# A four-layer decoder trunk: residual stream token-major, output products in 512-column matmuls

## The chip, the core and the metric

The kernel runs on one core of a Trainium2 chip. The metric is the device time of one execution in microseconds (us), lower is better. The engines are TensorE (PE, with its weight loads listed as PEld), VectorE (DVE), ScalarE (ACT), GpSimd (POOL) and SyncE (SP); here SP's queue issues the DMAs that bring the weights.

## The reference

A batch of one, 256 tokens, model width 1024, four layers, all in float32. Each layer has a token mixer (0: gMLP, 1: multi-head latent attention, MLA, 2: HGRN2, 3: gMLP again) and a convolutional FFN (2816 wide). A conditioning vector c gives every layer six vectors of 1024: shift, scale and gate for the mixer and for the FFN (adaLN).

```python
def rmsnorm(x, g):
    y = x * lax.rsqrt(jnp.mean(x * x, axis=-1, keepdims=True) + EPS)
    return y * g
...
for i in range(DEPTH):
    mod = c_act @ ada_w[i] + ada_b[i]
    sh1, sc1, g1, sh2, sc2, g2 = jnp.split(mod, 6, axis=-1)
    h = modulate(rmsnorm(x, mix_norm_g[i]), sh1, sc1)     # h * (1 + sc) + sh
    y = gmlp_mixer / mla_mixer / hgrn2_mixer (h, ...)     # each ends in "@ w_out"
    x = x + (1.0 + g1)[:, None, :] * y
    h = modulate(rmsnorm(x, ffn_norm_g[i]), sh2, sc2)
    x = x + (1.0 + g2)[:, None, :] * conv_ffn(h, ...)     # ends in "@ w_down"
return rmsnorm(x, final_g)
```

The last product of a mixer (go in gMLP, wo in MLA and HGRN2) and of an FFN (dn) is called an output product here: 1024 columns wide, with 2048, 1024 or 2816 rows to sum over. It is followed by the gate, the residual sum and the next norm.

## The kernel before, in words

The residual stream `x` lies feature-major: 128 partitions x 8 chunks of 128 features x 256 tokens. Every product is done in split form: a float32 operand is a high part in TensorE's fp32r type plus a low part, and `mm3` issues three matmuls (high by high, high by low, low by high; L239 to L241). Weights arrive as `raw` tiles of mostly 1 MB on SP's queue (`unit`, `want`, `dma_next`); ACT casts them to `wh` (L208) and DVE subtracts for `wl` (L209), 1024 columns at a time.

An output product of before takes weights of 128x128 as stationary operand and lets the 256 tokens move past. For each of the eight chunks of 128 output features a PSUM tile is finished, and `residual` (L458) does x += gate * product on DVE (L460), with the gate as a number for each partition. `square_chunk` squares the new chunk on ACT (L428; the last chunk on DVE, L426), and `stat_add` (L399) sums over features on TensorE, by short matmuls against ones into the tile `st`. When all eight are in, `rms_bc` (L407) takes the root (L409) and the reciprocal (L411), spreads the result over the partitions by TensorE (`bcn`, L416), and `modulate_chunk` (L440) makes the next product's operand `hh` and `hlo` chunk by chunk (DVE L444, ACT L445, DVE L446). The dn weights come as three pieces along the rows to sum over (8, 8 and 6 chunks of 128).

The adaLN vectors come in two ways, spread over the whole kernel as filler work: `ada_vector` (multiply and sum on DVE, L316) and `ada_tensor` (16 short matmuls `adaps` for a block, L294). `pacing` decides from the table RATE and from the count of units done how many of these steps each stage takes; `need` forces those that are wanted next. Blocks on TensorE that are still loaded run in the gap of a norm (`while loaded["p"]: ada_run("p")` in `modulated`).

The order of instructions on each engine is not the order of the source: a list scheduler with its own cost estimates sets it, within what the buffers allow (5 `raw` tiles, 10 of the pool "big", 3 "misc" and 4 "acc" PSUM banks). Engines then run their queues in order.

The stages in order: v, u, go (gMLP, layer 0), up, dn (FFN 0), MLA with wo, up, dn, HGRN2 with wo, up, dn, v, u, go (layer 3), up, dn, and the final norm. In what follows the gap ahead of a stage is the time from the last matmul of an output product to the first of the next product: up0 is the gap between go and up of layer 0, mix1 the one between dn of layer 0 and the mixer of layer 1, and so on.

Of the kernel before, what the change touches and what calls it, by code (L numbers as in the profile page):

```python
# [8 lines left out]
F32 = mybir.dt.float32  # L9
# [6 lines left out]
PSUM = bass.MemoryType.PSUM  # L16

# [17 lines left out]
OUTS = ((0, 0, 4), (0, 4, 4), (1, 0, 4), (1, 4, 4))  # L35
CONVAT = (3,)
SQACT = [3, 7]
# [9 lines left out]
STLAG = 3  # L47
# [4 lines left out]
        ("dn", 0): (0.0, 0.8), ("mix", 1): (1.85, 0.6), ("up", 1): (0.0, 0.2), ("dn", 1): (0.0, 0.85),  # L52
        ("mix", 2): (0.0, 0.4), ("lev", 2): (0.0, 0.25), ("hout", 2): (0.25, 1.05), ("up", 2): (0.0, 0.15),
        ("dn", 2): (0.0, 1.0), ("mix", 3): (0.0, 0.5), ("u", 3): (0.0, 0.3), ("go", 3): (0.0, 0.5),
        ("up", 3): (0.35, 0.0), ("dn", 3): (0.0, 0.7)}
# [6 lines left out]
for _name, _w in (("mix_g", 32), ("ada_b", 192), ("ffn_g", 32), ("final_g", 8), ("qg", 2), ("kvg", 1),  # L62
                  ("gmlb", 32), ("lb", 32), ("hgn", 1)):
    _COLS[_name] = _n
    _n += _w
# [27 lines left out]
def build(ctx, tc, A, out, stages=None):  # L93
# [8 lines left out]
    pp = ctx.enter_context(tc.tile_pool(name="pp", bufs=1, space=PSUM))  # L102

# [19 lines left out]
    x = one.tile([P, KC, S], F32, name="x")  # L123
    prm = one.tile([P, NPRM], F32, name="prm")
    for i in range(2):
        nc.sync.dma_start(x[:, 4 * i : 4 * i + 4, :], A["x"][:, 4 * i : 4 * i + 4, :])
    cin = one.tile([P, 8], F32, name="cin")
    nc.scalar.dma_start(cin[:], A["c"])
    n0, n1 = _COLS["ada_b"] + 48, _COLS["lb"]
# [3 lines left out]
    ident = one.tile([P, P], F32, name="ident")  # L133
# [3 lines left out]
    def late_consts():  # L137
        with tc.issue_after(state["lastdma"]):
            nc.sync.dma_start(prm[:, n1:], A["prm"][:, n1:])
            nc.sync.dma_start(ident[:], A["ident"])  # L140
# [12 lines left out]
    act.activation(cact[:], cin[:], AF.Silu)  # L153
# [94 lines left out]
    gate = one.tile([P, L, 2, 8], F32, name="gate")  # L248

    def mod_post(l, b0, n):  # L250
# [7 lines left out]
        elif part in (2, 5):  # L258
            dve.tensor_scalar_add(gate[:, l, part // 5, c : c + n], m, 1.0)
# [119 lines left out]
    def pacing():  # L379
# [3 lines left out]
        flush()  # L383
        for m in "pd":
# [22 lines left out]
    def rms_bc(ps, n, name, pieces=1):  # L407
# [5 lines left out]
        bc = [misc(f"bc{name}", (P, S // pieces)) for i in range(pieces)]  # L413
        for j in range(4):
            i, o = divmod(64 * j, S // pieces)
            pe.matmul(bc[i][:, o : o + 64], sel[:, j : j + 1].broadcast_to([P, P]), rs[:], start=True, stop=True)  # L416
        return bc[0] if pieces == 1 else bc

    cur = {"sq": []}

    def square_chunk(c):
        if c == 0:
            cur["st"] = stat_new("st")
        sq = t1("sq")[:]
        if c == KC - 1:
            dve.tensor_tensor(sq, x[:, c, :], x[:, c, :], op=ALU.mult)  # L426
        else:
            act.activation(sq, x[:, c, :], AF.Square)  # L428
        if c == 0:

            act.activation(sm("warm", 1)[:], sq[:, 0:1], AF.Sqrt)
        cur["sq"].append((sq, c))
        while len(cur["sq"]) > (STLAG if c < KC - 1 else 0):
            sq, i = cur["sq"].pop(0)
            stat_add(cur["st"], sq, i == 0, i == KC - 1)
# [4 lines left out]
    def modulate_chunk(l, which, c, bc):  # L440
        b = 24 * which + c
        sh = mod[:, l, b : b + 1]
        t = t1("nt")
        dve.scalar_tensor_tensor(t[:], x[:, c, :], amul[:, l, which, c : c + 1], bc, op0=ALU.mult, op1=ALU.mult)  # L444
        act.activation(hh[:, c, :], t[:], AF.Identity, bias=sh)  # L445
        dve.scalar_tensor_tensor(hlo[:, c, :], t[:], sh, hh[:, c, :].bitcast(F32), op0=ALU.add, op1=ALU.subtract)  # L446

    def modulated(l, which):
        bc = rms_bc(cur["st"], D, f"n{l}{which}")
# [3 lines left out]
        for c in range(KC):  # L453
            modulate_chunk(l, which, c, bc[:])
            if c in CONVAT:
                conv_half()

    def residual(l, which, c, ps):  # L458
        need(l, 2 + 3 * which)
        dve.scalar_tensor_tensor(x[:, c, :], ps, gate[:, l, which, c : c + 1], x[:, c, :], op0=ALU.mult, op1=ALU.add)  # L460
        square_chunk(c)
# [4 lines left out]

    def pair(name, apart):

        if apart:
            return [acc(f"{name}a", (P, S))[:], misc(f"{name}b", (P, S))[:]]  # L470
        t = acc(name, (P, 2, S))
        return [t[:, 0, :], t[:, 1, :]]
# [84 lines left out]
    def gmlp(l, j, start=None):  # L557
# [289 lines left out]
    class OutProj:  # L847


        def __init__(self, l, yh, yl):  # L850
            self.l, self.yh, self.yl = l, yh, yl
            self.ps = None

        def step(self, i):
            w = unit(LAST if i == 3 else None)
            if i == 0:
                self.ps = [v for t in range(4) for v in pair(f"wo{t}", False)]
            order = [(k, t) for k in range(2) for t in range(8)] if i < 3 else [(k, t) for t in range(8) for k in range(2)]
# [457 lines left out]
```

## Time and profile before

| | |
|---|---|
| runs of before | 1374.18 us median of 3 (1372.25 to 1375.31) |
| the profiled execution | 1373.39 us, span of its profile 1371.7 us |
| DMA | 326.22 MB, 238 GB/s over the span |
| instructions | 29075 |

The span is the stretch from the first to the last instruction in the profile; 1.7 us of the execution lie around it. In a row of the groups (line, engine, operation, out<-in, shapes, count) the first number behind the bar is the group's busy time, the second the mean of one in ns, and behind the next bar stands the idle time of the engine just before them and what ended it. In a row of the timeline the first number is the start in us, the second the duration; matmul durations overlap, so their pitch is read from the starts. Neighbours of one kind are joined in one row with a count.

### The profile page before, as it was taken

To read this page: it belongs to the slowest core of one execution; us is meant where nothing else is said; L and a number is where in the kernel's file an instruction comes from. 1 tells how busy PE (TensorE), PEld (TensorE's weight loads), DVE (VectorE), ACT (ScalarE), POOL (GpSimd) and SP (SyncE) were. 2 spreads that over 40 slices of the span, in tenths; PEclk is the share of its full clock that TensorE was granted. 3 is DMA by queue.
4 is the path that set the end of the run, shared out by engine and by line. 5 is a ranking of instruction groups with operands and counts; after the bars stand their busy time and mean duration, and the time that the engine had idled before them with its cause. 6 is when DMAs were issued, how large, how long until landed. Compare 5 with 4: busy or idle time off the path is not lost.

```text
span 1371.7 us, 29075 instructions
## 1 busy us (share of the span) xinstructions
PE 1339.3 (98%) x12244; PEld 1280.1 (93%) x12244; DVE 1107.8 (81%) x1788; ACT 770.8 (56%) x1202; POOL 17.0 (1%) x19
## 2 busy tenths in 40 slices
PE   8999999999999999999998999999999999999997
PEld 6799999999898899999897899999987999999997
DVE  5699788889787698897789978889877864888843
ACT  3764366664466666654666546665356543666633
POOL 0100000000000000000000000000001000000000
PEclk9999999999999999999999999999999999999999
DMA  9869955557957366588573756558958464455531
GB/s 383 333 246 336 386 203 192 197 211 314 382 214 278 117 253 215 228 317 348 204 258 125 297 222 247 212 181 325 361 186 303 176 234 164 158 181 184 185 124 32
DMA packets 49484, 326.22 MB, mean 238 GB/s; under 512 B 5957, under 2 KB 9029, under 8 KB 11975
## 3 DMA queue, kind: packets, MB, share of 16 engines
q1 hardware_dynamic: 47568, 322.72, 62.8%
q8 instruction: 96, 1.57, 0.5%
q10 hardware_dynamic: 1784, 1.65, 0.4%
q14 instruction: 36, 0.29, 0.1%
HBM read 323.29 MB, written 1.05 MB: 236 GB/s over the span
## 4 chain that ended last, share of the span: by engine, by line
PE 91%; DVE 4%; ACT 3%; DMA 1%; issue 1%; SPq 0%; DVEq 0%; ACTq 0%
PE up L240 12%; PE up L239 12%; PE up L241 12%; PE dn L239 5%; PE dn L240 5%; PE dn L241 5%; PE go L239 2%; PE go L240 2%; PE go L241 2%; PE u L240 2%; PE u L239 2%; PE u L241 2%; PE v L239 2%; PE v L240 2%; PE v L241 2%; DMA adaf<-ada 1%
## 5 line engine op out<-in xcount | busy, mean ns | idle before, releaser
L208 ACT CAST wh<-raw 128x1024 fp32r<-128x1024 f32 x426 | 434.8, 1032 | 390.2 <-PE up L240 170.9
L209 DVE TENSOR_TENSOR wl<-raw,wh 128x1024 fp32r<-128x1024 f32 x426 | 513.0, 1210 | 145.4 <-ACT wh L208 143.7
L239 PE MATMUL up<-hh,wh 128*128 128x256 f32 x1408 | 397.5, 283 | 2.6 <-ACT hh L445 2.5
L241 PE MATMUL up<-hh,wl 128*128 128x256 f32 x1408 | 397.4, 283 | 0.0
L240 PE MATMUL up<-hlo,wh 128*128 128x256 f32 x1408 | 397.3, 283 | 0.1
L239 PEld LDWEIGHTS up<-hh,wh 128*128 128x128 f32 x1408 | 269.7, 192 | 4.9 <-ACT hh L445 4.5
L240 PEld LDWEIGHTS up<-hlo,wh 128*128 128x128 f32 x1408 | 269.7, 192 | 0.6 <-DVE hlo L446 0.5
L241 PEld LDWEIGHTS up<-hh,wl 128*128 128x128 f32 x1408 | 270.0, 192 | 0.0
L316 DVE CUSTOM_DVE_ANT_0 adaw<-adaw,cbc,prm 128x1024 f32<-128x1024 f32 x120 | 152.1, 1278 | 2.3 <-DMA adaw<-adad 2.1
L239 PE MATMUL dn<-gh,wh 128*128 128x256 f32 x528 | 150.0, 284 | 3.0 <-ACT y L1095 3.0
L240 PE MATMUL dn<-gl,wh 128*128 128x256 f32 x528 | 149.4, 283 | 0.0
L241 PE MATMUL dn<-gh,wl 128*128 128x256 f32 x528 | 149.4, 283 | 0.0
L1095 ACT ACTIVATE y<-up,cwb 128x256 f32<-128x256 f32 x176 | 98.7, 561 | 11.4 <-DVE y L1097 11.3
L239 PEld LDWEIGHTS dn<-gh,wh 128*128 128x128 f32 x528 | 101.3, 192 | 3.7 <-ACT y L1095 3.3
L240 PEld LDWEIGHTS dn<-gl,wh 128*128 128x128 f32 x528 | 101.3, 192 | 0.0
L241 PEld LDWEIGHTS dn<-gh,wl 128*128 128x128 f32 x528 | 101.3, 192 | 0.0
L1097 DVE SCALAR_TENSOR_TENSOR y<-up,cwb,y 128x254 f32<-128x254 f32 x176 | 84.6, 481 | 4.8
L1096 DVE SCALAR_TENSOR_TENSOR y<-up,cwb,y 128x255 f32<-128x255 f32 x176 | 83.9, 477 | 0.5 <-ACT y L1095 0.4
L239 PE MATMUL u<-hh,wh 128*128 128x256 f32 x256 | 74.0, 289 | 0.0
L239 PE MATMUL go<-yh,wh 128*128 128x256 f32 x256 | 73.3, 287 | 0.0
L241 PE MATMUL u<-hh,wl 128*128 128x256 f32 x256 | 72.4, 283 | 0.0
L240 PE MATMUL u<-hlo,wh 128*128 128x256 f32 x256 | 72.4, 283 | 0.0
(340 smaller groups left out, 2457.4 us busy)
## 6 DMA issues: line engine op xcount, KB each, us to landing
raw<-up SPq DMA_DIRECT2D x88, 1024.0 KB, 4.8
adaw<-adad SPq DMA_DIRECT2D x60, 1024.0 KB, 7.0
raw<-dn SPq DMA_DIRECT2D x32, 1024.0 KB, 4.9
adaw<-adap SPq DMA_DIRECT2D x28, 1024.0 KB, 7.8
raw<-gmu SPq DMA_DIRECT2D x16, 1024.0 KB, 6.3
raw<-gmo SPq DMA_DIRECT2D x16, 1024.0 KB, 4.8
raw<-gmv SPq DMA_DIRECT2D x15, 1024.0 KB, 8.9
raw<-dn SPq DMA_DIRECT2D x16, 768.0 KB, 8.4
```

The lines of the kernel that those rows point to most:

```text
L208: act.copy(wh[:, :w], raw[:, o : o + w])
L209: i = dve.tensor_tensor(wl[:, :w], raw[:, o : o + w], wh[:, :w].bitcast(F32), op=ALU.subtract)
L239: pe.matmul(ps, lh, rh, start=start, stop=False)
L240: pe.matmul(ps, lh, rl, start=False, stop=False)
L241: i = pe.matmul(ps, ll, rh, start=False, stop=stop)
L316: dve.tensor_tensor_reduce(raw[:, e, :], raw[:, e, :], cbc[:], 1.0, prm[:, c0 : c0 + 1], ALU.mult, ALU.add, mod[:, l, b : b + 1])
L1095: act.activation(y[:], ps[:, e, :], AF.Identity, bias=b, scale=w[2])
L1096: dve.scalar_tensor_tensor(y[:, 1:], ps[:, e, : S - 1], w[1], y[:, 1:], op0=ALU.mult, op1=ALU.add)
L1097: dve.scalar_tensor_tensor(y[:, 2:], ps[:, e, : S - 2], w[0], y[:, 2:], op0=ALU.mult, op1=ALU.add)
```

## The change

The residual stream becomes token-major: `x` is 128 partitions (tokens) x 2 token halves t x 1024 features.

- Output products (`out_product`): 128x128 blocks of activations (features x 128 tokens) are stationary, and 512 weight columns move. The four combinations of token half t and column half f have a PSUM bank each. In all units but the last the loop runs over the weight chunks with t and f inside; in the last unit it finishes one (t, f) after the other. The weights of go and dn are packed for it; dn now has 11 units of 1 MB (8 of 1 MB and 4 of 0.75 MB before), and its paces in RATE are scaled to that. In the last dn the final two units are merged.
- Gates: a gate is now a row along the features and has to stand on all partitions. `gate_row` puts the gate's 8 columns into a cleared tile (POOL), adds one, transposes blocks of 32x32 (both DVE) and stores the result by four DMAs of 8x32 to device memory; `gate_load` reads it back, spread over 128 partitions, into the tile `gx` (pool "big").
- `residual(t, f)`: DVE multiplies 512 columns by the gate (`gated`) and adds them to x; ACT squares with its accumulator, which gives the sum of squares for each token. After f = 1: `root` (ACT square root and DVE reciprocal of one column) and `scaled` (x times the reciprocal root into `gx`, half on DVE, half on ACT).
- `turned`: 16 transposes of 128x128 on TensorE put the scaled x back feature-major, into PSUM tiles `xt`; `modulate_chunk` reads them. The matmuls `st` and `bcn` of these norms go away.
- The final norm multiplies by a row of final_g loaded by a DMA; the first norm uses accumulators of ACT and DVE; `ident` is loaded at the start.

```diff
+    def gate_row(l, which, m):
+        g = t1("gcol", 32)
+        pool.memset(g[:], 0.0)
+        dve.tensor_scalar_add(g[:, 0:8], m, 1.0)
+        r = t1("grow", 32)
+        dve.transpose(r[:], g[:])
+        row = dp.tile([8, 4, 32], F32, name=f"gate{l}{which}")
+        for j in range(4):
+            nc.sync.dma_start(row[:, j, :], r[32 * j : 32 * j + 8, :])
+        grows[l, which] = row
...
+        gx = cur["gx"] = big("gx", (P, 2, D))
+        row = grows.pop((l, which))
+        nc.sync.dma_start(gx[:, 1, :], row[:].rearrange("c j i -> (c j i)").unsqueeze(0).broadcast_to([P, D]))
...
+    def scaled(t, rs):
+        xn = cur["gx"][:, t, :]
+        dve.tensor_scalar_mul(xn[:, 0:512], x[:, t, 0:512], rs)
+        i = act.activation(xn[:, 512:D], x[:, t, 512:D], AF.Copy, scale=rs)
...
+    def turned(c, w, bank=misc):
+        ps = bank("xt", (P, w, S))
+        for e in range(w):
+            for t in range(2):
+                pe.transpose(ps[:, e, t * P : t * P + P], cur["gx"][:, t, (c + e) * P : (c + e) * P + P], ident[:])
+        return ps
...
-        dve.scalar_tensor_tensor(t[:], x[:, c, :], amul[:, l, which, c : c + 1], bc, op0=ALU.mult, op1=ALU.mult)
-        act.activation(hh[:, c, :], t[:], AF.Identity, bias=sh)
-        dve.scalar_tensor_tensor(hlo[:, c, :], t[:], sh, hh[:, c, :].bitcast(F32), op0=ALU.add, op1=ALU.subtract)
+        dve.tensor_scalar(t[:], xt, amul[:, l, which, c : c + 1], mod[:, l, b : b + 1], op0=ALU.mult, op1=ALU.add)
+        split(hh[:, c, :], hlo[:, c, :], t[:])
...
-    def residual(l, which, c, ps):
-        need(l, 2 + 3 * which)
-        dve.scalar_tensor_tensor(x[:, c, :], ps, gate[:, l, which, c : c + 1], x[:, c, :], op0=ALU.mult, op1=ALU.add)
-        square_chunk(c)
+    def residual(t, f, ps, last):
...
+        dve.tensor_tensor(g[:], ps, gx[:, 1, s], op=ALU.mult)
+        dve.tensor_tensor(x[:, t, s], x[:, t, s], g[:], op=ALU.add)
+        act.activation(g[:], x[:, t, s], AF.Square, accum_out=ss[:, 2 * t + f : 2 * t + f + 1])
...
+        if f == 0:
+            if t == 0:
+                act.activation(sm("warm", 1)[:], ss[:, 0:1], AF.Sqrt)
+            dve.tensor_scalar(ss[:, 4 + t : 5 + t], ss[:, 2 * t : 2 * t + 1], 1.0 / D, EPS, op0=ALU.mult, op1=ALU.add)
+        else:
+            rs = root(t, ss[:, 6:8], ss[:, 2 * t + 1 : 2 * t + 2], ss[:, 4 + t : 5 + t])
...
+                scaled(t, rs)
...
+    def out_product(name, k0, units, yh, yl, last, fin_=False):
...
+        def one_(kc, t, f):
+            a, b = hl(units[(kc - k0) // 2], kc % 2 * D + 512 * f, 512)
+            ts = slice(t * P, t * P + P)
+            mm3(ps[2 * t + f][:], yh(kc)[:, ts], yl(kc)[:, ts], a, b, kc == 0, kc == last)
...
         pace("go", l)
+        gate_load(l, 0)
         for i in range(8):
             w = unit(LAST if i == 7 else None)
-            ps = acc(f"go{i}", (P, S))
-            for k in range(16):
-                a, b = hl(w, k * P, P)
-                mm3(ps[:], a, b, yh(k), yl(k), k == 0, k == 15)
-                if k == 7:
-                    flush(mid=1)
-            residual(l, 0, i, ps[:])
+            out_product("go", 2 * i, [w], yh, yl, 15)
```

How the change moves instructions shows at three places. The first is DVE at the end of go in layer 0 (in the rows: `x<-go` and `gated<-go` are residual steps, `wl<-raw` weight conversions, `nt` and `hlo` the norm's output, `adaw,mod` an adaLN step; numbers behind names count the tiles). Before, from the last weights of go to the first nt:

```order
L209 TENSOR_TENSOR wl_0_1920<-raw_1849,wh_0_1919 128x1024
L209 TENSOR_TENSOR wl_1024_1924<-raw_1849,wh_1024_1923 128x1024
L209 TENSOR_TENSOR wl_0_1989<-raw_1917,wh_0_1988 128x1024
L460 SCALAR_TENSOR_TENSOR x<-go_1930,gate,x 128x256
L209 TENSOR_TENSOR wl_1024_1993<-raw_1917,wh_1024_1992 128x1024
L460 SCALAR_TENSOR_TENSOR x<-go_1996,gate,x 128x256
L426 TENSOR_TENSOR sq<-x 128x256
L411 RECIPROCAL rsn_2072<-sdn_2070 128x64
L209 TENSOR_TENSOR wl_0_2120<-raw_1986,wh_0_2119 128x1024
L444 SCALAR_TENSOR_TENSOR nt<-x,amul,bcn_2074 128x256
```

And in the changed kernel, in two pieces that leave out rows between:

```order
L500 TENSOR_TENSOR gated<-go_1517,gx 128x512
L210 TENSOR_TENSOR wl_0_1773<-raw_1733,wh_0_1772 128x1024
L210 TENSOR_TENSOR wl_1024_1777<-raw_1733,wh_1024_1776 128x1024
L501 TENSOR_TENSOR x<-x,gated 128x512
L500 TENSOR_TENSOR gated<-go_1518,gx 128x512
```

```order
L501 TENSOR_TENSOR x<-x,gated 128x512
L448 RECIPROCAL ss<-ss 128x1
L509 TENSOR_SCALAR ss<-ss 128x1
L455 TENSOR_SCALAR gx<-x,ss 128x512
L448 RECIPROCAL ss<-ss 128x1
L455 TENSOR_SCALAR gx<-x,ss 128x512
L339 ISA adaw_0_0_1931,mod<-adaw_0_0_1931,cbc,prm 128x1024
L339 ISA mod 128x1
L473 TENSOR_SCALAR nt<-xt,amul,mod 128x256 x3
```

The residual steps, spread over the stage before, now all stand at its end; the two conversions of the first up weights stand between the first `gated` and its `x`, and an adaLN step stands ahead of the first nt.

The second place is TensorE at the same point. Before, from the last matmul of go to the first of up:

```order
L241 MATMUL go_1996<-yh_885,wl_1024_1924 128x256
L401 MATMUL st<-sq,ones 32x64 x12
L294 MATMUL adaps<-adaw_5_0_1518,cact 32x256 x5
L401 MATMUL st<-sq,ones 32x64 x4
L294 MATMUL adaps<-adaw_5_0_1518,cact 32x256 x3
L294 MATMUL adaps<-adaw_5_1_1591,cact 32x256 x5
L416 MATMUL bcn_2074<-rsn_2072,sel 128x64 x4
L294 MATMUL adaps<-adaw_5_1_1591,cact 32x256 x3
L294 MATMUL adaps<-adaw_5_2_1657,cact 32x256 x8
L239 MATMUL up_2153<-hh,wh_0_1988 128x256
```

And after:

```order
L241 MATMUL go_1520<-wl_1024_1740,yh_869 128x512
L242 MATMUL go_1520<-wh_1024_1739,yl_870 128x512
L464 MATMUL xt<-ident,gx 128x128 x16
L240 MATMUL up_1933<-hh,wh_0_1772 128x256
L240 MATMUL up_2005<-hh,wh_0_1899 128x256
```

The adaLN blocks that stood in the gap have moved into the go stage (further up in the queue, between go's matmuls), and the gap holds the transposes alone.

The third is ACT between dn of layer 0 and the mixer of layer 1 (`wh<-raw` are weight casts). Before:

```order
L428 ACTIVATE sq<-x 128x256 x2
L208 CAST wh_1024_4450<-raw_4382 128x1024
L428 ACTIVATE sq<-x 128x256 x3
L409 ACTIVATE sdn_4518<-st,epsc 128x64
L208 CAST wh_0_4543<-raw_4444 128x1024
L208 CAST wh_1024_4565<-raw_4444 128x1024
L208 CAST wh_0_4637<-raw_4563 128x1024
L445 ACTIVATE hh<-nt,mod 128x256 x8
```

And after:

```order
L502 ACTIVATE gated,ss<-x 128x512 x2
L447 ACTIVATE ss<-ss 128x1
L502 ACTIVATE gated,ss<-x 128x512
L456 ACTIVATE gx<-x,ss 128x512
L447 ACTIVATE ss<-ss 128x1
L456 ACTIVATE gx<-x,ss 128x512
L209 CAST wh_0_4041<-raw_3939 128x1024
L559 CAST hh<-nt 128x256
```

The half of `scaled` for the first tokens stands between the last square and the second root, and one weight cast is left ahead of the first hh where three stood.

More of the change, by code (lines that the diff above doesn't have):

```diff
@@ L412, in rms_bc @@
         state["chain"] = (getattr(i0, "ins", i0), getattr(i1, "ins", i1))
-        bc = [misc(f"bc{name}", (P, S // pieces)) for i in range(pieces)]
+        bc = misc(f"bc{name}", (P, S))
         for j in range(4):
[L415 to L435, printed above, removed]
+            pe.matmul(bc[:, 64 * j : 64 * j + 64], sel[:, j : j + 1].broadcast_to([P, P]), rs[:], start=True, stop=True)
@@ L450, in modulated @@
+        late = misc if which == 0 and l % 3 == 0 else acc
+        xts = [turned(*i) for i in tiles[:3]]
         while loaded["p"]:
@@ new lines, in build, with finish @@
+    fin = {}
+    def finish(t, rs):
+        y = fin["y"]
+        for f in range(2):
+            s = slice(512 * f, 512 * f + 512)
+            if t == 0:
+                dve.scalar_tensor_tensor(y[:, t, s], x[:, t, s], rs, fin["g"][:, s], op0=ALU.mult, op1=ALU.mult)
+            elif f == 0:
+                dve.tensor_scalar_mul(y[:, t, s], y[:, t, s], rs)
+            else:
+                act.activation(y[:, t, s], y[:, t, s], AF.Copy, scale=rs)
+            (nc.scalar if f else nc.sync).dma_start(out[:, t, s], y[:, t, s])
```

196 lines of the change are left out of this document (105 added, 91 removed).

## The prediction, made before the changed kernel ran

> **What bounds the kernel now.** I read the page's head first (busy shares, clock, chain), then the timeline for the pitch of matmuls, the groups for counts, the windows by stage, and the timeline between stages.
>
> ```profile
> span 1371.7 us, 29075 instructions
> PE 1339.3 (98%) x12244; PEld 1280.1 (93%) x12244; DVE 1107.8 (81%) x1788; ACT 770.8 (56%) x1202; POOL 17.0 (1%) x19
> PEclk9999999999999999999999999999999999999999
> DMA  9869955557957366588573756558958464455531
> PE 91%; DVE 4%; ACT 3%; DMA 1%; issue 1%; SPq 0%; DVEq 0%; ACTq 0%
> ```
>
> TensorE is busy 98%, at a granted clock of 0.9 or more in every slice, and carries 91% of the chain that ends last. Time goes away where matmuls go away or come closer together, and comes back wherever TensorE waits. DVE, at 81% on average, is the engine that could follow it.
>
> Two stretches of the timeline give the pitch: of 256 moving columns (the output product go), and of 512 (the product v).
>
> ```profile
> 129.77 0.28 PE L239 MATMUL go<-yh,wh 128*128 128x256 f32 x1
> ...
> 133.37 0.28 PE L239 MATMUL go<-yh,wh 128*128 128x256 f32 x1
> 1042.22 0.39 PE L239 MATMUL v<-wh,hh 128*128 128x512 f32 x1
> ...
> 1045.62 0.39 PE L239 MATMUL v<-wh,hh 128*128 128x512 f32 x1
> ```
>
> The first two starts are 30 matmuls apart: 3.60/30 = 0.1200 us each. The other two are 15 apart: 3.40/15 = 0.2267 us. Two small ones cost 0.2400, one large one 0.2267, so each pair that becomes one saves 13.3 ns. The product v has just the changed form, activations stationary and 512 weight columns moving.
>
> **The change, part by part.** *Fewer, longer matmuls.* The groups give the counts; each row is one of three lines alike, dn3b has a row like dn3a's, the other layer's wo one like this.
>
> ```profile
> L239 PE MATMUL go<-yh,wh 128*128 128x256 f32 x256 | 73.3, 287 | 0.0
> L239 PE MATMUL dn<-gh,wh 128*128 128x256 f32 x528 | 150.0, 284 | 3.0 <-ACT y L1095 3.0
> L239 PE MATMUL dn3a<-gh,wh 128*128 128x256 f32 x88 | 25.3, 288 | 0.0
> L240 PE MATMUL wo<-hyl,wh 128*128 128x256 f32 x64 | 18.1, 284 | 0.0
> ```
>
> 3 × (256 + 528 + 2×88 + 2×64) = 3264 matmuls become 1632: 1632 × 13.3 ns = **−21.8 us**, all on TensorE.
>
> *The statistics leave TensorE.* Inside a stage each residual chunk brought 8 of these short matmuls (a group's first row counts neighbours too):
>
> ```profile
> 365.49 0.28 PE L241 MATMUL dn<-gh,wl 128*128 128x256 f32 x1
> 365.70 0.43 PE L401 MATMUL st<-sq,ones 128*32 128x64 f32 x16
> 366.06 0.39 PE L239 MATMUL dn3a<-gh,wh 128*128 128x256 f32 x1
> ```
>
> Here 16 keep dn's matmuls 0.57 us apart where 0.12 is usual: 0.45 us, 0.23 for 8. A go stage has seven such groups ahead of its last matmul (1.69 us by its length beyond 384 pitches), a dn stage about four (0.85): 2×1.69 + 4×0.85 = **−6.8 us**.
>
> *Supply.* The stages get shorter, but their weights, casts and adaLN products do not get fewer. Windows on go0, dn0 and dn2 (columns: length, then PE, PEld, DVE, ACT, POOL busy, clock, DMA share, GB/s):
>
> ```profile
> 124.60:172.50 47.90, 47.90 (x419) 47.00 (x417) 37.59 (x52) 19.01 (x25) 0.00 (x0) 1.00 0.97 370
> 306.10:370.40 64.30, 64.30 (x554) 63.85 (x552) 54.02 (x88) 28.61 (x40) 0.00 (x0) 1.00 0.88 350
> 945.90:1012.00 66.10, 64.62 (x554) 63.97 (x553) 56.05 (x87) 30.72 (x44) 0.00 (x0) 1.00 0.86 327
> ```
>
> go0 holds 192 of the 1632 pairs (2.56 us) and 1.69 us of statistics, so it should lose 4.25 us. But DMA stands at 0.97 there, and the three adaLN blocks on TensorE (48 adaps, 3 us) that ran in the gap behind it now stand inside it. Bounds: 0 and 4.25 lost again; I take **+3.5**, near the upper, because of the 0.97. Each dn stage should lose 264 × 13.3 ns + 0.85 = 4.4 us. DVE's 54.0 us, with residual steps of 0.69 where 0.48 stood, then fill about 55 of 59.9 us in dn0 (92%), 57 of 61.7 in dn2, and 350 GB/s becomes 350×64.3/59.9 = 376, above go0's 370. Bounds: 0 and 4.4 each for dn0 to dn2; I take 0.8, 1.2 and 1.5, nearer none since neither engine is yet full: **+3.5**. In the MLA layer the product is mixed with attention, and half its saving hangs on DVE: **+0.6**. dn3, go3 and wo2 have slack and keep theirs.
>
> *The gaps.* After each output product comes a norm, during which the next product cannot start. The first of seven gaps, and the ends of the last:
>
> ```profile
> 172.42 0.28 PE L241 MATMUL go<-yh,wl 128*128 128x256 f32 x1
> 172.74 0.48 DVE L460 SCALAR_TENSOR_TENSOR x<-go,gate,x 128x256 f32<-128x256 f32 x1 [4.58 <-PE go L241]
> 174.22 0.32 ACT L409 ACTIVATE sdn<-st,epsc 128x64 f32<-128x64 f32 x1 [6.73 <-PE st L401]
> 174.56 0.55 DVE L411 RECIPROCAL rsn<-sdn 128x64 f32<-128x64 f32 x1 [0.88 <-ACT sdn L409]
> 175.49 1.23 DVE L209 TENSOR_TENSOR wl<-raw,wh 128x1024 fp32r<-128x1024 f32 x1 [0.38 <-ACT wh L208]
> 176.64 0.48 DVE L444 SCALAR_TENSOR_TENSOR nt<-x,amul,bcn 128x256 f32<-128x256 f32 x1
> 177.25 1.36 ACT L445 ACTIVATE hh<-nt,mod 128x256 fp32r<-128x256 f32 x3
> 177.81 0.63 PE L239 MATMUL up<-hh,wh 128*128 128x256 f32 x3
> ...
> 1164.96 0.28 PE L241 MATMUL go<-yh,wl 128*128 128x256 f32 x1
> 1170.36 0.50 PE L239 MATMUL up<-hh,wh 128*128 128x256 f32 x2 [0.98 <-ACT hh L445]
> ```
>
> 5.39 us in the first, 5.40 in the last, 41.8 in all seven (mix1 5.31, up1 6.97, mix2 6.39, up2 6.77, mix3 5.61 between them). Durations for what takes the place of this chain:
>
> ```profile
> L645 DVE TENSOR_TENSOR gt<-sv,gr 128x512 f32<-128x512 f32 x16 | 11.0, 686 | 6.2 <-PE sv L639 6.2
> L576 ACT ACTIVATE jk<-v,nsh 128x512 f32<-128x512 f32 x16 | 11.4, 716 | 0.8 <-DVE nsh L580 0.7
> L576 ACT ACTIVATION_READ_ACCUMULATOR jk<-v,nsh 128x1 f32 x16 | 3.0, 190 | 0.0
> L464 ACT CAST yh<-u 128x512 fp32r<-128x512 f32 x16 | 9.9, 619 | 17.7 <-DVE u L646 17.7
> L815 PE MATMUL pt<-ident,e 128*128 128x128 f32 x24 | 4.0, 275 | 0.0
> L807 DVE TENSOR_SCALAR e<-e,su 128x256 f32<-128x256 f32 x8 | 2.8, 348 | 0.1
> L464 ACT CAST gh<-g 128x256 fp32r<-128x256 f32 x88 | 35.4, 403 | 14.0 <-DVE g L1101 14.0
> L316 DVE CUSTOM_DVE_ANT_0 adaw<-adaw,cbc,prm 128x1024 f32<-128x1024 f32 x120 | 152.1, 1278 | 2.3 <-DMA adaw<-adad 2.1
> ```
>
> From the last matmul's start: 0.42 until its product stands (0.32 above, plus the 0.11 by which 512 columns run longer), 0.69 gated, 0.69 x, 0.72 + 0.19 square, 0.3 sqrt (sdn 0.32), about 0.2 reciprocal of one column, 0.6 for scaled(0)'s ACT half, which the order puts ahead of the second sqrt, and some 0.15 in DVE's queue: 3.96 us. Then scaled(1) 0.62, transposes and handoffs 0.3, nt 0.35, hh 0.40, and those weight casts (near 1.0 us each: their DVE partner above is 1.23) that the order puts ahead of the first hh. One cast gives 6.0, each more about 1.0: mix1 6.0, up1 7.0 (two), mix2 8.0 (three, with two adaLN steps on DVE), up2 6.5, mix3 7.0 (two), up3 6.0. Sum 40.5, against 36.4 now: **+4.0**. Bounds: −4 (no cast in the way anywhere) and +10 (a cast and an adaLN step more in each).
>
> up0 is its own case. The order puts two wl of up0's first weights between the first gated and its x, and an adaLN step of 1.28 + 0.08 us ahead of nt. Two wl are 2.46 us, so x(1,1) is done near 6.0 us, the second reciprocal near 8.0, and hh starts near 10.5: **+5.0**. Bounds: 0, if those weights land early enough for both wl to run before the first product ends, and +7. TensorE has 16 transposes there and nothing else.
>
> ```profile
> 1361.57 0.28 PE L241 MATMUL dn3b<-gh,wl 128*128 128x256 f32 x1
> 1365.74 1.54 SPq L1133 DMA_DIRECT2D out<-fo  x2
> 1368.00:1371.70 3.70, 0.00 (x0) 0.00 (x0) 0.00 (x0) 0.00 (x0) 0.00 (x0) 0.50 0.62 185
> ```
>
> The last row is the windows' on the tail: with TensorE idle the granted clock was 0.50. If up0's gap brings the same, the first matmuls after it run slower; no gap of this trace is long enough to show it, so I leave it to the range. The Trainium skill (TensorE: Matmul & The Clock Gate, Part 1: The HAM clock gate) says that an idle window of about 3.4 us halves the clock, and that it takes as much sustained work to get it back. The trace agrees on the halving. By that page half of 3.4 us, some 1.7 us (an estimate), would come on top, and the sum below would be −11.3.
>
> *Tail.* The last matmul to the first output DMA's issue took 4.17 us; statistics, broadcast and the four products of fo fall away, while the longer residual and one scaling come in. The last half is issued about 4.95 us after instead of 5.9: **−1.0**. Bounds ±1.
>
> *What costs nothing.* Gates: 8 times a POOL memset, two small DVE steps, four 8x32 stores and one broadcast load of 512 KB on SP's queue, issued units ahead of the residual that reads them; their cover is the stage itself. If SP stands at a full buffer first, the load is late and the first residual waits. The load adds 4 MB, 1% of the traffic. The start is ruled by weights arriving (the DMA row above begins with 0.9 and 0.8), so its new norm moves it by 0 to 1. A larger dn unit (11 of 1 MB for 12) changes bytes by nothing.
>
> *Sum:* −21.8 − 6.8 + 3.5 + 3.5 + 0.6 + 4.0 + 5.0 − 1.0 = **−13.0 us**. The sum stands against the profiled execution (span 1371.7, 1373.4 in all), 0.8 below the median of the runs: 1360.4, and so **1361** in their measure.
>
> **The rivals.** *A: everything saved is kept.* DVE and DMA still have room in all four stages, and gaps but up0's stay as they are: −13.0 − 7.6 − 4.0 = −24.6, or 1349.6, and 1344.6 if up0's two wl come early. For it: DVE's queue is not full by any row. Against: 0.97 in go0. Chance 0.14.
>
> *B: the stages keep their length.* go0 and dn0 to dn2 are set by what DVE and DMA deliver, and shorten by nothing: 0.75 + 3×4.4 − 3.5 = 10.4 more, −2.6, or 1371.6, at the edge of no change. For it: 370 GB/s in go0. Against: dn2 runs at 327. Chance 0.08.
>
> *C: slower, by the gaps.* What the order does at up0, two wl ahead of the first x, happens by waiting in all seven gaps: 5 us each is 35 instead of 9, +13, 1387. It decides from 22 us of growth in all gaps. For it: the new chain has four DVE and four ACT steps after the last matmul in in-order queues. Against: elsewhere the order shows one to three casts and no wl. Chance 0.07.
>
> *D: the long matmul saves nothing.* If the fixed part of a matmul were not paid twice by two small ones here, the long form would take 2 × 0.1200 and the −21.8 would fall away: +8.8, or 1383. The rows of v, 0.2267 us in the very form, speak against it; that these operands come from other tiles speaks for it, weakly. Chance 0.02. The Trainium skill (the same page, Back-to-back issue gap) gives N/2.4 + 2.5 ns for an isolated matmul of N columns at full clock; by it only 1632 × 2.5 ns = 4.1 us would go, the sum would be +4.7 (an estimate), and the rows of v do not agree with it.
>
> **How the numbers follow.** The forecast has 0.69; its own range, from the bounds of supply and gaps, is 1352 to 1370. Faster by over 0.2% (2.7 us, about what a measurement of this kernel can tell from no change): forecast and A, 0.83. Within 0.2%: B, 0.08. Slower: C and D, 0.09. For 8 in 10 the range takes in A's first figure and B's: 1348 to 1371.
>
> **What would show it.** Pitch: output products 0.227 us apart, 1632 of them. Statistics: no st beside the norms inside attention and HGRN2, no bcn. Supply: go0 near 47 us from first to last start, dn0 near 60.7, with waits for wl or raw in them; if they are 43.5 and 59.9, A is right. Gaps: 6 to 8 us, up0 near 10.5 with two wl ahead of the first x; below 6 everywhere means that I mis-sized the chain. The clock after up0's gap. The prediction fails low if supply keeps up, and high if a gx load or a gate row comes late, since then every residual waits.

## The result: slower by 0.85%, and the profile after

The changed kernel takes 1385.45 us (median of 4 runs, 1384.09 to 1386.61) against 1373.59 us of the kernel before: a ratio of 1.0085, 95% interval 1.0068 to 1.0103. Forecast were 1361 us (1348 to 1371) and a faster kernel. Its profiled execution took 1384.63 us, 1382.8 of them in the span. The head of its page:

```profile
span 1382.8 us, 24847 instructions
PE 1329.4 (96%) x10092; PEld 1195.7 (86%) x10092; DVE 1123.6 (81%) x1818; ACT 776.2 (56%) x1220; POOL 18.0 (1%) x27
PEclk8999999999999999999999999999999999999999
PE 56%; DVE 9%; ACT 2%; issue 1%; ACTq 0%; DVEq 0%
```

TensorE works 10 us less than before, and is without work for 53.4 us of the span where it was 32.4. DVE's share of the chain that ends last went from 4% to 9%, although the shares of that chain add up to only 68% of the span here. Four rows of TensorE's list of waits (engine and line, what it waited for, us in total, times, longest):

```profile
PE dn L240 <- DVE y L1171: 11.8, 5, 4.5
PE xt L464 <- DVE gx L455: 8.6, 6, 5.4
...
PE up L240 <- DVE y L1171: 2.4, 6, 0.4
...
PE dn L240 <- ACT y L1169: 1.4, 1, 1.4
```

The list of before had 3.0 us for dn waiting on y, in two waits, and the row of dn among the forecast's counts shows them. y is the convolution's step in the FFN's up stage; it reads the up product out of PSUM. The stage lengths tell where that stands (us, first start to last start in the timeline; a gap is last start to next first start, "up1 to dn1" the end of up to the end of dn):

| | before | after | change | forecast |
|---|---|---|---|---|
| start and v0 | 71.14 | 72.18 | +1.0 | 0 |
| go0 | 47.77 | 48.92 | +1.2 | -0.8 |
| gap up0 | 5.39 | 9.84 | +4.5 | +5.0 |
| six other gaps | 36.45 | 41.03 | +4.6 | +4.0 |
| dn0, dn3 | 128.43 | 119.56 | -8.9 | -8.0 |
| MLA with wo1 | 80.92 | 82.65 | +1.7 | -0.7 |
| up1 | 126.96 | 130.90 | +3.9 | 0 |
| up1 to dn1 | 66.10 | 71.63 | +5.5 | -3.2 |
| dn2 | 65.98 | 69.80 | +3.8 | -2.9 |
| HGRN2 with wo2 | 149.38 | 147.58 | -1.8 | -1.3 |
| go3 | 47.76 | 43.42 | -4.3 | -4.3 |
| tail | 10.1 | 8.3 | -1.8 | -1.0 |

The rest (up0, up2, up3, v3 and u3) adds 1.7. go3, dn0 and dn3 show the whole saving that was worked out. dn1 and dn2, which by the pitch and the statistics alone should have lost 4.4 us each, got longer by 5.5 and 3.8.

What happens there is on TensorE and DVE in the 20 us after up1. TensorE first (start, duration; the bracket is the idle time before and who ended it):

```profile
600.92 0.28 PE L242 MATMUL up<-hh,wl 128*128 128x256 f32 x1
602.63 0.47 PE L240 MATMUL dn<-wh,gh 128*128 128x512 f32 x1 [1.43 <-ACT y L1169]
...
605.91 0.39 PE L242 MATMUL dn<-wh,gl 128*128 128x512 f32 x1
610.82 0.77 PE L240 MATMUL dn<-wh,gh 128*128 128x512 f32 x1 [4.53 <-DVE y L1171]
...
616.17 0.39 PE L242 MATMUL dn<-wh,gl 128*128 128x512 f32 x1
618.00 0.47 PE L240 MATMUL dn<-wh,gh 128*128 128x512 f32 x1 [1.45 <-DVE y L1171]
...
623.02 0.47 PE L240 MATMUL dn<-wh,gh 128*128 128x512 f32 x1 [0.39 <-DVE y L1171]
```

Four waits, with 15 matmuls of dn between two of them. An up bank holds a pair of chunks, and DVE makes two steps of y for each chunk (L1170, L1171). DVE in the same time, the last y of each of the four last pairs (602.00, 610.19, 617.38, 622.39), and all that stands between 607.00 and the second of them:

```profile
602.00 0.48 DVE L1171 SCALAR_TENSOR_TENSOR y<-up,cwb,y 128x254 f32<-128x254 f32 x1
...
607.00 0.48 DVE L1171 SCALAR_TENSOR_TENSOR y<-up,cwb,y 128x254 f32<-128x254 f32 x1
607.39 1.28 DVE L339 CUSTOM_DVE_ANT_0 adaw<-adaw,cbc,prm 128x1024 f32<-128x1024 f32 x1
608.60 0.09 DVE L339 DVE_READ_ACCUMULATOR2_ANT mod<- 128x1 f32 x1
608.60 0.48 DVE L1170 SCALAR_TENSOR_TENSOR y<-up,cwb,y 128x255 f32<-128x255 f32 x1
608.99 1.28 DVE L339 CUSTOM_DVE_ANT_0 adaw<-adaw,cbc,prm 128x1024 f32<-128x1024 f32 x1
610.19 0.09 DVE L339 DVE_READ_ACCUMULATOR2_ANT mod<- 128x1 f32 x1
610.19 0.48 DVE L1171 SCALAR_TENSOR_TENSOR y<-up,cwb,y 128x254 f32<-128x254 f32 x1
...
617.38 0.48 DVE L1171 SCALAR_TENSOR_TENSOR y<-up,cwb,y 128x254 f32<-128x254 f32 x1
...
622.39 0.48 DVE L1171 SCALAR_TENSOR_TENSOR y<-up,cwb,y 128x254 f32<-128x254 f32 x1
```

These four steps, each 0.48 us long, end 0.15 us ahead of TensorE's four starts. (The bracket of the first start names a step of y on ACT that ended at the same moment.) dn now has four accumulators from its first unit on, each a bank of the pool "acc", which has four banks; up rotates through the same four. So dn's bank 0 comes free with the last y of the fourth pair from the end, bank 1 with the third, and so on. The order on TensorE shows it from the other side: 15 matmuls for the first accumulator (all that the five converted weight tiles allow), then the next accumulator.

```
L240 MATMUL dn_6688<-wh_0_6718,gh_5062 128x512
L241 MATMUL dn_6688<-wl_0_6719,gh_5062 128x512
L242 MATMUL dn_6688<-wh_0_6718,gl_5063 128x512
L240 MATMUL dn_6689<-wh_0_6602,gh_5062 128x512
```

And since all five weight tiles are then held until the last bank has used them, no further weights can be converted; DVE's queue was filled with adaLN steps instead. The kernel before had DVE as late there: its last y of layer 1 ended 23.6 us behind up1's last matmul, at 614.1 us; here it is 22.0. But there one PSUM bank of dn sufficed for the first two of eight output chunks, some 5.8 us of matmuls, and one wait was left, for the second bank:

```profile
596.27 0.28 PE L241 MATMUL dn<-gh,wl 128*128 128x256 f32 x1
598.04 0.36 PE L239 MATMUL dn<-gh,wh 128*128 128x256 f32 x1 [1.48 <-ACT y L1095]
```

dn0 and dn3 take four banks in the same way and do not wait: there the last y ends 6.9 us behind up's last matmul. The resource was in the diff, the wait in a row of the forecast, and the forecast priced neither.

### The profile page after: what moved, and what is told of

The parts are those of the page before. It is cut to its first block, busy times and chain, and to the rows that moved or that the text cites. A ratio compares the mean times of both kernels' runs of the same rounds, so it can differ in the third digit from the quotient of the medians.

```text
span 1382.8 us, 24847 instructions
## 1 busy us (share of the span) xinstructions
PE 1329.4 (96%) x10092; PEld 1195.7 (86%) x10092; DVE 1123.6 (81%) x1818; ACT 776.2 (56%) x1220; POOL 18.0 (1%) x27
## 4 chain that ended last, share of the span: by engine, by line
PE 56%; DVE 9%; ACT 2%; issue 1%; ACTq 0%; DVEq 0%
PE up L240 8%; PE up L241 8%; PE up L242 8%; PE dn L240 4%; PE dn L242 4%; PE dn L241 4%; DVE adaw L339 2%; DVE wl L210 1%; PE wo L240 1%; ACT wh L209 1%; PE wo L242 1%; PE wo L241 1%; PE v L240 1%; PE v L242 1%; PE v L241 1%
## 5 line engine op out<-in xcount | busy, mean ns | idle before, releaser
L240 PE MATMUL dn<-wh,gh 128*128 128x512 f32 x352 | 139.5, 398 | 13.3 <-DVE y L1171 11.8
L241 PE MATMUL dn<-wl,gh 128*128 128x512 f32 x352 | 139.1, 395 | 0.6 <-DVE wl L210 0.6
L242 PE MATMUL dn<-wh,gl 128*128 128x512 f32 x352 | 139.2, 395 | 0.0
L240 PEld LDWEIGHTS dn<-wh,gh 128*128 128x128 f32 x352 | 67.5, 192 | 29.9 <-issue 12.5
L1171 DVE SCALAR_TENSOR_TENSOR y<-up,cwb,y 128x254 f32<-128x254 f32 x176 | 84.7, 481 | 5.0
L1170 DVE SCALAR_TENSOR_TENSOR y<-up,cwb,y 128x255 f32<-128x255 f32 x176 | 84.0, 477 | 2.5 <-ACT y L1169 2.5
L241 PEld LDWEIGHTS dn<-wl,gh 128*128 128x128 f32 x352 | 67.4, 191 | 14.9 <-DVE wl L210 1.1
L242 PEld LDWEIGHTS dn<-wh,gl 128*128 128x128 f32 x352 | 67.2, 191 | 14.3
L240 PE MATMUL v<-wh,hh 128*128 128x512 f32 x128 | 51.9, 408 | 3.0 <-ACT hh L559 2.5
```

The source lines that it names most:

```text
L240: pe.matmul(ps, lh, rh, start=start, stop=False)
L241: pe.matmul(ps, lh, rl, start=False, stop=False)
L242: i = pe.matmul(ps, ll, rh, start=False, stop=stop)
L1170: dve.scalar_tensor_tensor(y[:, 1:], ps[:, e, : S - 1], w[1], y[:, 1:], op0=ALU.mult, op1=ALU.add)
L1171: dve.scalar_tensor_tensor(y[:, 2:], ps[:, e, : S - 2], w[0], y[:, 2:], op0=ALU.mult, op1=ALU.add)
```

## The experiments

Two theories and the forecast's rival B as a third stood for dn1 and dn2: the banks, the adaLN steps in DVE's queue, and the supply of weights. The first two runs separate them.

**Two accumulators from other banks (run banks).**

```diff
-            cur["ps"] = [acc(f"{name}{i}") for i in range(4)]
+            cur["ps"] = [(misc if name == "dn" and i < 2 else acc)(f"{name}{i}") for i in range(4)]
```

> Edit: of dn's four accumulators the two of token half 0 come from the three "misc" PSUM banks, and two instead of four from the "acc" banks that the up product rotates through. Theory 1 (banks): in the changed kernel dn needs four acc banks within its first 2 us, and each is still held by one of the last four up chunks until its convolution steps (y) have run; so dn1's waits (1.4, 4.5, 1.5, 0.4 us, with some 2 us at half clock behind them) and dn2's (3.0, 2.5 us) go to under 2 us a stage, dn1 and dn2 come from 69.9 and 69.8 to 62 to 64.5 us, and the time from 1385 to about 1373 (1370 to 1376). Theory 2 (adaLN): y is late because adaLN steps stand between the y steps in VectorE's queue; these steps stay, so dn1 and dn2 stay within 1.5 us of 69.9 and the time at 1383 to 1386. Theory 3 (supply): dn1 and dn2 lack weights; nothing changes, 1385.

Measured: 1367.79 us, ratio to before 0.9955 (0.9940 to 0.9970): 17.7 us gone by where two PSUM tiles come from. From the end of up1 to the end of dn1 it takes 59.65 us instead of 71.63, dn2 62.77 instead of 69.80. The window on 590 to 660 us (columns as in the forecast's windows) shows TensorE without a pause, beside a VectorE that is 91% busy:

```profile
590.00:660.00 70.00, 70.00 (x356) 58.25 (x358) 63.53 (x96) 33.36 (x47) 0.00 (x0) 1.00 0.91 364
```

The adaLN steps still stand between the y steps, and the last y of layer 1 ends 26.2 us behind up1's last matmul, later than in the changed kernel. Theory 1 holds, theory 2 and theory 3 fall for these stages; the gain was larger than theory 1 said, since dn1 lost its waits altogether.

**No adaLN loads in dn's first four units (run late_adaln).**

```diff
+            if l in (1, 2):
+                state["rate"]["d"] = 0.0 if i < 4 else RATE["dn", l][1] * 11 / 7
```

> Edit: in dn of layers 1 and 2 no adaLN loads are issued in the first four of eleven units, and accordingly more in the other seven; accumulators as in the changed kernel. Theory 1 (banks): the y steps come earlier, so the four banks come free earlier: dn1 and dn2 fall to about 64 to 66 us, time about 1376 to 1379. Theory 2 (adaLN): the waits vanish, dn1 and dn2 at 62 to 63.5, time 1371 to 1374. Theory 3 (supply): the same work in fewer units makes VectorE the bound there, dn1 and dn2 stay near 70 or grow, time 1385 or more.

Measured: 1375.18 us. dn1 takes 64.96 and dn2 67.11 us. The waits of dn on y are halved, and not gone:

```profile
PE dn L240 <- DVE y L1171: 6.4, 2, 3.4
```

The adaLN steps lengthen the wait; the banks make it. The time lies just below theory 1's range and above theory 2's, dn2 above both.

**The pitch undone (run cols256).**

```diff
-            mm3(ps[2 * t + f][:], yh(kc)[:, ts], yl(kc)[:, ts], a, b, kc == 0, kc == last)
+            for h in range(2):
+                hs = slice(256 * h, 256 * h + 256)
+                mm3(ps[2 * t + f][:, hs], yh(kc)[:, ts], yl(kc)[:, ts], a[:, hs], b[:, hs], kc == 0 and h == 0, kc == last and h == 1)
```

> Edit: each 512-column matmul of an output product is issued as two of 256 columns, everything else as in the changed kernel. If a pair saves 13.3 ns on TensorE, stages bound by TensorE get longer by their number of pairs: dn0 and dn3 by 264 x 13.3 ns = 3.5 us, go3 by 2.6 us, and all 1632 pairs by 21.8 us at most: 1385 becomes 1401 to 1407, the lower figure if waits in go0, dn1 and dn2 swallow part. If the long form saves only 2.5 ns a pair (the rival of the forecast), 1387 to 1390.

Measured: 1397.50 us, 12.05 more than the changed kernel, less than expected. By stage the price is as forecast: dn0 63.40 against 59.78, dn3 63.39 against 59.78, go3 46.04 against 43.42, which is 9.85 us for 720 pairs, 13.7 ns each. The total fell short because other places moved: 22 of go0's 48 adaps now ran in the gap behind it, so that go0 took 48.70 us, although its 192 pairs should have added 2.6 to 48.92; the two wl steps no longer stood between go0's residuals, and the gap up0 was 7.41 us instead of 9.84; the gap mix1 was 5.64 instead of 7.89. A whole-kernel difference alone would have given the pair 7.4 ns.

**No look-ahead at go0's end (run go0_lookahead).**

```diff
-            w = unit(LAST if i == 7 else None)
+            w = unit((1 if l == 0 else LAST) if i == 7 else None)
```

> Edit: in the last unit of go in layer 0 the first up weights are not converted ahead, so that their two wl steps (2.35 us) no longer stand between the first gated and its x on VectorE. Theory 1: these two steps delay the whole norm; the gap up0 falls from 9.84 to 7.0 to 7.8 us, the time by 2 to 3 us to 1382.5, less if the first up matmuls then wait for their wl. Theory 2: the gap is set by the ten steps of the new chain itself, and the conversions only move behind it; the gap plus up0 stay within 0.7 us, time 1385.

Measured: 1393.04 us, above what either theory gave. The gap up0 fell to 7.87 us, near theory 1's figure, but up0 grew from 128.5 to 135.4: TensorE now waited in it for the late casts and wl. The two conversions do delay the norm, but they have to be done before it. The trace of after says how: ahead of the first gated DVE waits 7.71 us with nothing to do, while the conversions stand behind it in the queue.

```profile
172.34 0.69 DVE L500 TENSOR_TENSOR gated<-go,gx 128x512 f32<-128x512 f32 x1 [7.71 <-PE go L242]
172.94 2.35 DVE L210 TENSOR_TENSOR wl<-raw,wh 128x1024 fp32r<-128x1024 f32 x2
175.21 0.68 DVE L501 TENSOR_TENSOR x<-x,gated 128x512 f32<-128x512 f32 x1
...
181.91 1.28 DVE L339 CUSTOM_DVE_ANT_0 adaw<-adaw,cbc,prm 128x1024 f32<-128x1024 f32 x1
```

**Conversions first (run banks_wlfirst).** This and the next three stand on top of banks (1367.79 us).

```diff
+        with contextlib.ExitStack() as es:
+            if t == f == 0:
+                es.enter_context(tc.issue_after(state["sub"]))
             dve.tensor_tensor(g[:], ps, gx[:, 1, s], op=ALU.mult)
```

> Edit on top of the run banks: the first gated of every output product is issued after the weight conversions that are already due, so that the two wl steps stand ahead of it on VectorE, not between it and its x. In the trace of after VectorE waits 7.7 us for that gated while the casts it needs are long done. Theory: the conversions then cost nothing and the gaps whose order had them between lose 2.3 to 2.5 us each: up0 9.84 to 7.4, mix3 9.36 to 7.0; time 1367.8 to about 1363. Rival: the weights land so late that gated now waits for them, and the gap stays at 9.8 or grows; time 1368 or more.

Measured: 1364.12 us, 3.7 less; the kernel before, measured beside these four, was 1372.82 us where it had been 1374.07 beside banks, so differences to banks are uncertain by about 1.3 us. The gap up0 is 8.02, mix3 7.71 us: 1.7 to 1.8 us less each instead of 2.4.

**No adaLN in up1 (run banks_up1_noadaln).** `("up", 1): (0.0, 0.2)` becomes `(0.0, 0.0)`.

> Edit on top of banks: no adaLN loads are issued in up of layer 1 (rate 0.2 set to 0); later stages take them over. Theory: the cluster of three adaLN steps in mid-up1 pushed the order of ScalarE by one weight cast, so that each convolution step stands behind one more cast and TensorE waits 0.57 us in each of the last six pairs of chunks; without it up1 goes from 130.9 to 127.0 us, the time from 1367.8 to 1364 to 1366, as HGRN2 takes over the steps. Rival: the slip comes from the gate row or the larger pool's buffers; up1 stays at 130.9 us.

Measured: 1367.83 us, no change. up1 did come down to 127.10 us, so the adaLN steps are what pushed the order there; but up2, with eight of these steps instead of six, now took 131.59 us instead of 126.97, and the gap mix2 grew from 8.38 to 12.47, with four of them among its norm's steps on DVE instead of two. The work has to be done somewhere, and here the new places cost what the old one had.

**A warm start (run banks_warm).** `WARM = 12` becomes `WARM = 26`.

> Edit on top of banks: 26 instead of 12 matmuls on ones at the start, so that TensorE is busy until the first product's operands come. In the trace of after TensorE is idle from 5.5 to 9.0 us and the clock stands at 0.50 from 9 to 15 us. Theory: with the clock at 1.00 the first adaLN block and the transposes take half as long, v0 starts at 12.8 to 13.5 us instead of 14.3; the start is bound by DMA until about 45 us, so the end of v0 moves by less than 0.8 us, the time by 0 to 0.8 us. Rival: v0's end moves by the full 1 to 1.5 us.

Measured: 1368.37 us. The granted clock is 1.00 throughout the start, v0 starts at 12.48 us instead of 14.30, and ends at 70.37 instead of 72.06: the rival is right, the start is not bound by DMA alone. The time did not fall, because HGRN2 took 150.09 instead of 147.74 us in this kernel's order. That the two are related was not shown.

**adaLN blocks back in the gaps (run banks_gapfill).**

```diff
-        while loaded["p"]:
-            ada_run("p")
+        with tc.issue_after(state["mm"]):
+            while loaded["p"]:
+                ada_run("p")
```

> Edit on top of banks: the adaLN blocks on TensorE that are meant for a norm's gap are issued after the last matmul of the output product, in the gap, as in the kernel before. Theory: go0 loses the 48 adaps (3.0 us) that stand in it: 48.9 to 46.0 us, gap up0 unchanged since TensorE idles there; the same for what stands in dn2; time 1367.8 to 1364. Rival (the forecast's): go0 is set by DMA at 0.98, so that it shortens by under 1 us; time 1367.

Measured: 1359.15 us, 8.6 less. go0 fell from 48.92 to 43.42 us, more than the 3.0 us of the theory, dn2 (which had 26 adaps in it) from 62.77 to 59.64, and the gap up0 stayed at 9.84. The window on go0 in after, of the adaps matmuls alone (length, then PE, PEld, DVE busy, clock, DMA share, GB/s):

```profile
125.60:174.70 49.10, 4.44 (x48) 1.07 (x48) 0.00 (x0) 1.00 0.98 386
```

And the whole stage in this run, with ACT and POOL behind DVE:

```profile
125.60:169.30 43.70, 43.70 (x197) 35.90 (x199) 35.12 (x46) 14.72 (x15) 0.00 (x0) 1.00 0.98 394
```

The DMA share is 0.98 in both, and the stage is 5.5 us shorter with it. The share said that the queues had work, not that the stage waited for it.

**Alone on the changed kernel (run gapfill_alone).** The same edit without the banks:

> The changed kernel with the adaLN blocks of TensorE put back into the gaps, nothing else. Theory: go0 falls from 48.9 to 43.4 us as in banks_gapfill and the gap up0 stays at 9.84; dn1 and dn2 keep their waits for banks (69.9, 69.8); time 1385.5 to 1379 or 1380. Rival: without the bank edit the blocks were hidden in other waits, and the time falls by less than 3 us.

Measured: 1379.59 us. go0 43.42, gap up0 9.85, dn1 69.91, dn2 69.75: each stage as expected.

**The clock in dn's wait (run hold_clock).** 14 matmuls on ones behind dn's first three, in layers 1 and 2 of the changed kernel:

```diff
+                        if name == "dn" and kc == 0 and (t, f) == (0, 1) and cur["hold"]:
+                            hold = misc("hold", (P, P))
+                            with tc.issue_after(state["mm"]):
+                                for _ in range(14):
+                                    i = pe.matmul(hold[:], onesw[:], onesw[:], start=True, stop=True)
+                            es.enter_context(tc.issue_after(getattr(i, "ins", i)))
```

> The changed kernel with 14 matmuls on ones behind the first three of dn in layers 1 and 2, so that TensorE works 3 us longer ahead of its longest wait for a bank (4.5 us in dn1, 3.0 us in dn2). Theory: the clock fell to a half because TensorE stood still for over 2.5 us; with a wait of about 1.5 us and less it stays at 1.00, the matmuls behind it run 0.227 us apart instead of 0.427, dn1 loses 2.0 us (69.9 to 67.9), dn2 1.8 us, the time 3 to 4 us to 1382. Rival: the slow matmuls come from operands or DVE's traffic, not from standing still; the pitch of 0.427 us stays, and the time is 1385 or more.

Measured: 1385.97 us, nothing gained. The windows of after on its wait of 4.5 us and on the matmuls behind it:

```profile
605.90:610.80 4.90, 0.40 (x2) 0.01 (x1) 4.90 (x10) 1.32 (x3) 0.00 (x0) 0.76 0.80 284
610.80:615.20 4.40, 4.38 (x10) 3.46 (x11) 4.40 (x8) 0.40 (x1) 0.00 (x0) 0.50 1.00 425
```

Those of this run, on what is left of that wait (1.4 us), the matmuls behind it, and the next wait:

```profile
607.00:611.00 4.00, 2.60 (x12) 1.85 (x11) 4.00 (x7) 1.20 (x3) 0.00 (x0) 1.00 0.91 301
611.00:615.00 4.00, 2.86 (x13) 2.01 (x11) 4.00 (x10) 0.41 (x1) 0.00 (x0) 1.00 1.01 428
615.00:618.00 3.00, 0.64 (x2) 0.57 (x3) 2.86 (x7) 1.54 (x4) 0.00 (x0) 0.84 1.02 426
```

The half clock behind the first wait is gone, so it came from standing still. But the next bank came free when it did before, with DVE's y; the wait for it grew from 1.45 to 3.50 us, and the clock fell there. Here the slow matmuls had cost nothing, since another wait stood behind them.

**Three edits together, and four (runs three_edits, four_edits).** banks, wlfirst and gapfill:

> The changed kernel with three edits together: two of dn's accumulators from other banks (banks), conversions ahead of the first gated (wlfirst), adaLN blocks in the gaps (gapfill). Theory: the three act in different stages and add up: banks -17.7, gapfill -8.6, wlfirst -3.7 from 1385.5 give 1355.5 (1354 to 1358), with go0 at 43.4, gap up0 at 8.0, dn0 to dn3 at 59.6 to 60 apart from dn1's earlier start. Rival: the adaLN blocks in the gaps and the earlier conversions take the same time, so that wlfirst gives nothing on top of gapfill: 1359.

Measured: 1356.51 us, ratio to before 0.9881 (0.9866 to 0.9896); its parts added up to within the expected range. All four dn stages are at the saving, go0 at 43.42, gap up0 at 8.03. The head of its page:

```profile
span 1353.5 us, 24838 instructions
PE 1315.5 (97%) x10092; PEld 1190.9 (88%) x10092; DVE 1121.8 (83%) x1818; ACT 774.8 (57%) x1220; POOL 17.9 (1%) x27
```

TensorE is without work for 38.0 us. The longest total in its list of waits is now the norm's:

```profile
PE xt L464 <- DVE gx L455: 7.1, 8, 1.8
```

With the warm start as a fourth:

> As three_edits, and 26 instead of 12 matmuls on ones at the start. Theory: v0 starts and ends 1.7 us earlier, as in banks_warm, where HGRN2's order gave it back by chance; time 1354 (1352.5 to 1356). Rival: the start is bound by DMA and a later stage waits for its weights instead; time as three_edits.

Measured: 1357.34 us, no better: v0 ends 2.8 us earlier than in three_edits, and HGRN2 takes 149.91 instead of 146.10 us. This happened in both kernels with the warm start; what in HGRN2 gives it back stays open.

## Why the prediction was wrong, point by point

- **Pitch and statistics (−21.8 and −6.8): right.** dn0 lost 4.43, dn3 4.44, go3 4.34 us where 4.4, 4.4 and 4.25 were worked out, and cols256 gave the pair back at 13.7 ns. Rival D is out, and the rule of the Trainium skill beside it (TensorE: Matmul & The Clock Gate, Back-to-back issue gap) does not agree with the rows: 2.5 ns a pair by it, 13.7 measured.
- **Gaps (+4.0 and +5.0): right in sum, in part by luck.** Measured were +4.6 and +4.5. The parts scatter (mix1 7.89 for 6.0, mix3 6.59 for 7.0). In mix1 the granted clock stood at 0.50 for 3.4 us behind the pause of 2.11 us; behind the same pause it held in late_adaln and hold_clock, and there mix1 is 6.38 and 6.37. The two wl steps were where the order had shown them, and took 2.35 us, of which banks_wlfirst got 1.8 back. The clock did fall in up0's gap, from 178.3 to 185.2 us, but up began at 184.5: three of its matmuls ran slowly, which is 0.4 us in place of the 1.7 that the forecast left to its range.
- **Supply in dn1 and dn2 (1.2 and 1.5): the step that failed.** What was lost of the saving is 9.9 and 8.2 us, 15.4 more than forecast. The forecast read it as a question of how full DVE and DMA are; dn lost its time waiting for PSUM banks that the last up pairs still held, 7.8 us in the four waits of dn1 alone. The banks run had VectorE fuller (91% around dn1 where after had 82%), lost nothing in dn1 and 1.2 us in dn2. The step left out the PSUM banks, though the row of dn that it counted from ends with a wait for one (3.0 us on y): it counted what the new matmuls cost and not what they hold.
- **Supply in go0 (+3.5): a number near, for the wrong reason.** 5.4 was lost, and not to the DMA: the 48 adaps cost all of it, 115 ns each in among the go matmuls, where the forecast had priced them at 3 us and named them beside the DMA. banks_gapfill took it all back at the same share of 0.98.
- **Not foreseen:** up1 +3.9 (TensorE waits there six times for y, and with that stage's adaLN loads moved on, in banks_up1_noadaln, the waits are gone; that one weight cast too early on ScalarE is the link was not tested), MLA +2.4 against its term (not taken apart here), and the start +1.0, for which "0 to 1" stood in the text and 0 in the sum (from 7.6 to 17.9 us the granted clock was 0.50 here and 1.00 before; at 1.00, in banks_warm, v0 ends 1.7 us earlier than in banks).
- **Tail −1.8 for −1.0, HGRN2 −1.8 for −1.3, dn0 without its 0.8:** on the good side.

Together: 15.4 + 3.9 + 1.9 (go0) + 2.4 + 1.0, with 1.7 for up0, up2, up3 and layer 3, less 0.8, 0.8 and 0.5, and 0.1 by the gaps, give 24.3, which takes −13.0 to 11.3; the spans are 11.1 us apart, the rest is rounding.

Of the rivals, C had the sign and the time (1387) with 0.07, but its mechanism did not happen: the gaps grew by 9.1 us in all, not 35. B named the right stages for a wrong cause. A, "everything saved is kept", is what the three edits come near to: 16.5 us under the kernel before, where A had 24.6.

## What to carry to other kernels

When a change makes a product use more accumulators at once, write down for each of its PSUM banks who read it last and when that reader ends; a bank is a resource of the stage before. Filler work belongs where the engine stands still anyway: check on which side of the last matmul the order puts it. And test a share near 1 by taking work away from the stage, before calling it the bound; price a change by its stages, since a list scheduler moves several us elsewhere with each edit.

## What the runs showed of the hardware

The length of a pause does not tell whether the granted clock falls. In after, TensorE paused for 2.95 us ahead of dn2's second bank; the clock was still 1.00 when it went on, and 1.2 us later the pitch went from 0.23 to 0.43 us for some 3 us:

```profile
969.00 0.47 PE L240 MATMUL dn<-wh,gh 128*128 128x512 f32 x1 [2.95 <-DVE y L1171]
969.30 0.40 PE L241 MATMUL dn<-wl,gh 128*128 128x512 f32 x1
...
970.65 0.63 PE L240 MATMUL dn<-wh,gh 128*128 128x512 f32 x1
971.08 0.63 PE L241 MATMUL dn<-wl,gh 128*128 128x512 f32 x1
...
973.64 0.39 PE L241 MATMUL dn<-wl,gh 128*128 128x512 f32 x1
```

In late_adaln a pause of 2.98 us ahead of dn1's second bank left it at 1.00. What the traces show instead is a fixed grid. The stretches of after with a granted clock of 0.50 between the start and the tail begin at 178.32, 376.30, 608.40, 680.08, 970.22 and 977.04 us; these are 58, 68, 21, 85 and 2 steps of 3.413 us apart, and each stretch is one or two such steps long. Four steps of after, then three of late_adaln (columns as in the forecast's windows):

```profile
966.80:970.22 3.42, 1.22 (x5) 1.05 (x6) 3.42 (x9) 0.21 (x1) 0.00 (x0) 1.00 0.60 208
970.22:973.63 3.41, 3.41 (x9) 2.65 (x8) 3.41 (x8) 0.41 (x1) 0.00 (x0) 0.50 1.01 425
973.63:977.04 3.41, 0.89 (x4) 0.48 (x3) 2.85 (x7) 1.32 (x3) 0.00 (x0) 1.00 0.86 356
977.04:980.46 3.42, 3.42 (x9) 2.68 (x9) 2.71 (x7) 1.27 (x3) 0.00 (x0) 0.50 0.91 352
603.94:607.35 3.41, 2.05 (x10) 1.35 (x8) 3.25 (x7) 0.28 (x2) 0.00 (x0) 1.00 1.01 423
607.35:610.76 3.41, 1.79 (x8) 1.52 (x9) 2.60 (x6) 1.69 (x5) 0.00 (x0) 1.00 1.02 430
610.76:614.18 3.42, 3.42 (x16) 2.25 (x15) 2.69 (x7) 1.69 (x5) 0.00 (x0) 1.00 0.81 335
```

TensorE is idle for 2.2 and 2.5 us in the first and third step of after, and a step at half clock follows each. The pause of late_adaln is split between two steps, with 1.4 and 1.6 us idle, and none follows. In all fourteen traces, from 100 to 1345 us, no step at full clock with less than 1.55 us idle was followed by half clock, and every one with more than 1.76 us was; between these two figures both happened. So the same pause costs or not by where it falls on the grid, which differs from run to run.

The step agrees with the free-running window of about 3.4 us in the Trainium skill (TensorE: Matmul & The Clock Gate, Part 1: The HAM clock gate); that a step idle for about half of its length suffices is less than the idle window that it states.
